# Three gate groups traced among branch C's tiles instead of branch A's

## The chip, the cores and the metric

The kernel runs on one core of one Trainium2 chip. The metric is the device time of one execution in microseconds (us). Three timed runs of the kernel before gave 2320.02, 2320.87 and 2327.75 us; their median, 2320.87 us, is what the changed kernel is compared with. The profile comes from a further execution, which took 2326.91 us.

## What is computed

Two transformer-like layers run one after the other on a sequence of 1024 tokens with 1024 features. The change lies in the first, which has four branches. Each branch yields y of 256 columns, which is gated, multiplied by a projection and weighted by a sigmoid gate taken from the layer's input h:

```
y_a = nsa_attention(...)               # branch A (index 0): compressed, selected and window attention
y_b = banded_attention(..., sink)      # branch B (index 1)
y_c = stick_breaking_attention(...)    # branch C (index 2): sigmoids and a cumulative product over the keys
y_d = retention(...)                   # branch D (index 3)
for i, (y, z) in enumerate(branches):
    yi = y * silu(z)
    term = sigmoid(h @ w_merge[i]) * (yi @ w_br[i])
    merged = term if merged is None else merged + term
x = x + gate * (merged @ w_out)
```

The selection in branch A picks 16 of 16 blocks at this length, so that its selected attention is causal attention over all keys. The second layer (a convolution, an attention, a pooling, an MLP) is not touched.

## The kernel before, in words

All large products are made three times over, with the operands split in a high and a low part (lines 229 to 231: high by high, high by low, low by high), each matmul 128 by 128 on 512 columns. Attention works in tiles of 128 queries. A branch treats its four heads as two pairs, and for each pair goes over eight tiles of queries, tile i seeing i+1 blocks of 128 keys. Tile (1, 5) below is pair 1, i = 5.

Branch A's tile (`tile_of` in `branch_a`) makes scores on TensorE (PE; L804, L806; for the compressed keys L1041, L1042), adds a bias and takes the maximum on VectorE (DVE; L845), exponentials on ScalarE (ACT; L857), the reciprocal and the normalisation on DVE (L865, L150), transposes on PE (L276), copies the transposed probabilities out as high part on ACT (L147) and low part on DVE (L157, tile PT), multiplies them with the values on PE (L823) and sums the result on DVE (L833, L834; `join`). It does so for the selected and for the window attention. Branch C's tile makes two sigmoids on ACT (L1108, L1109), masks on GpSimd (POOL; L1111), a scan on DVE (L1113), a product on DVE or POOL (L1115), and then the same transposes, copies and products.

Between the tiles stands work that does not depend on them: fillers. `attend` asks a table after each tile which to trace: `m` is one group of a merge (`fill`), `g` one gate group (`pre`), `q` the query products of pair 1, `z` the gate of a finished pair.

```
            for i in range(NT):
                with stream(_T["ST1"], -1000000):
                    tile_of(p, i, ops[p])
                for c in works.get((p, i), ""):
                    todo[c]()
```

The tables are `FA`, `FB` and `FC` in `_T`, for the branches A, B and C, and `FD` for branch D. A gate group works out sigmoid(h @ w_merge) ahead for one branch and a quarter of the columns: two weight loads of 512 KB (SP's queue) and their split in high and low parts (ACT, DVE, POOL), four products of 24 matmuls each into a PSUM bank named mm, a tanh on ACT for each, and a store of 256 KB to DRAM, which the merge loads later. The groups are taken in a fixed order from `pre_todo`: the four of branch A's gate, then branch C's. There are two mm banks; gate groups, merges and projections share them.

A scheduler places the instructions of each engine in one fixed order when the program is built. Tiles stand in a stream of higher priority, so that a filler goes where the tiles leave an engine free by the scheduler's own reckoning. The order of the branches is D, A, C, B. A merge is queued when its branch is done: that of A gives the fillers `m` of branch C. Where a gate has been worked out ahead, the merge makes only the product with w_br (6 matmuls in place of 24 more).

Of the kernel before, what the change touches and what calls it, by code (L numbers as in the profile page):

```python
# [17 lines left out]
P = 128  # L18
# [6 lines left out]
SLOPES = [2.0 ** -2, 2.0 ** -4, 2.0 ** -6, 2.0 ** -8]  # L25
QS = 0.125

_T = dict(STA='s', XN1=0, PWT=1, PO='0x1', PO2={}, PS=2, PSX=0, PSE='a', PB=99, PEA=(0, 1, 4), WB=8, XL=3, CLO='v', STE=None, STW=None, ST1='b', ST2='b', PLP='pvv', WLO2='v', QXP=1, LW='vp', LEAD=10, FD={0: 'g', 1: 'b', 6: 'g'}, FW=(0, 2), AG=0, PREO=(0, 2, 1), PMB=0, PWB=1, PM=3, SG=2, FA={(0, 2): 'g', (0, 3): 'mmm', (0, 7): 'qm', (1, 0): 'gg', (1, 6): 'gz'}, FB={(0, 3): 'm', (0, 7): 'qm', (1, 3): 'm', (1, 5): 'z', (1, 7): 'm'}, FC={(0, 3): 'mm', (0, 7): 'q', (1, 3): 'zm', (1, 6): 'm'}, NORM='v', NORM2='v', CS=4, CSB=8, MM=2, SB=2, TB=3, OB=1, WHI='aaav', WLO='pv', PTH='a', NW=9, NBLK=31, PTB=2, XN=1, AS=(2, 4, 6, 7), CPP=2, CALT=1, WORK='s0 A A A A A A A A p s1 q t c B c B c B c B c 0a 1a P w 5 4 6 7 g 2 3a e u c B e c B c e B c c e B 1b 0b 3b', KS=(2, 0, 3, 1))


_C1 = [("trel", 1024), ("wrel", 640), ("crel", 256), ("brel", 128), ("brel2", 128), ("dm", 512), ("xi", 256), ("zeta", 256)]
# [2081 lines left out]
```

## Time and profile before

| | us |
|---|---|
| median of three timed runs | 2320.87 |
| the profiled execution | 2326.91 |
| its span, first to last instruction | 2325.2 |
| PE busy in the span | 2239.4 |
| DVE busy in the span | 1517.2 |
| ACT busy, POOL busy | 966.2, 474.8 |

The span is what lies between the first and the last instruction that the profile records. A PE shown as busy is not at its peak: the next matmul starts before the one in front has ended. So what counts is the distance between starts, and an engine's idle time with what ended it. Branch A's tiles stand at about 279 to 640 us, branch C's at about 640 to 840 us, and branch B's follow.

### The profile page before, as it was taken

The page shows a single profiled execution, that of the slowest core. Times are in us where ns is not written, and L with a number is a line of the kernel's source. Part 1 is how long each engine was busy: PE and PEld are TensorE (multiplying, and loading weights), DVE is VectorE, ACT ScalarE, POOL GpSimd, SP SyncE. Part 2 cuts the span into 40 slices and gives each one's busy share as a digit, 9 for nine tenths or more (in the row PEclk, how much of TensorE's full clock was granted, in tenths as well). Part 3 has the DMA queues.
Part 4 walks back from the last instruction along what each step waited for, and adds up shares of the span by engine and source line. Part 5 has one row for each costly group of instructions (what it writes and reads, how often), then busy time and mean ns, then how long its engine had stood idle before and what let it go on. Part 6 is the DMA issues. An engine that isn't in the chain of part 4 may idle for free.

```text
span 2325.2 us, 30286 instructions
## 1 busy us (share of the span) xinstructions
PE 2239.4 (96%) x11004; PEld 1860.3 (80%) x11004; DVE 1517.2 (65%) x2955; ACT 966.2 (42%) x1941; POOL 474.8 (20%) x404
## 2 busy tenths in 40 slices
PE   8999999999989999999998999899999999999998
PEld 6788888888877778877887787677788888888877
DVE  7634466665677965623579876866576678578684
ACT  6211344444455544422322344634545454344452
POOL 4222100010155622112330000012034340000021
PEclk8999999999999999999999999999999999999999
DMA  9421221121132333224221211156565687525313
GB/s 319 165 90 61 63 69 50 46 89 62 32 109 84 116 119 106 73 82 145 103 71 28 82 50 37 37 172 212 159 192 180 203 324 248 176 90 163 109 55 118
DMA packets 202783, 272.72 MB, mean 117 GB/s; under 512 B 17086, under 2 KB 126214, under 8 KB 202634
## 3 DMA queue, kind: packets, MB, share of 16 engines
q1 hardware_dynamic: 194240, 257.95, 34.3%
q10 hardware_dynamic: 8394, 12.84, 1.8%
q8 instruction: 87, 1.43, 0.3%
q14 instruction: 62, 0.51, 0.1%
HBM read 199.43 MB, written 71.32 MB: 116 GB/s over the span
## 4 chain that ended last, share of the span: by engine, by line
PE 82%; DVE 9%; DMA 3%; ACT 2%; POOL 2%; issue 2%; SPq 0%; POOLq 0%; DVEq 0%; ACTq 0%
PE mm L229 15%; PE mm L230 15%; PE mm L231 15%; PE t L276 4%; PE o L823 3%; DVE blk L1342 2%; PE s L1682 2%; PE s L1684 2%; PE s L1683 2%; PE t L2028 1%; PE t L2029 1%; PE t L2027 1%; PE mm L2028 1%; PE t L1682 1%; PE mm L2029 1%
## 5 line engine op out<-in xcount | busy, mean ns | idle before, releaser
L229 PE MATMUL mm<-blk,wh 128*128 128x512 f32 x1264 | 506.2, 401 | 20.8 <-DVE tz L1157 6.2
L230 PE MATMUL mm<-blk,wh 128*128 128x512 f32 x1264 | 500.6, 396 | 0.0
L231 PE MATMUL mm<-blk,wl 128*128 128x512 f32 x1264 | 499.1, 395 | 0.3 <-DVE wl L157 0.3
L229 PEld LDWEIGHTS mm<-blk,wh 128*128 128x128 f32 x1264 | 238.7, 189 | 74.3 <-DVE tz L1157 9.2
L231 PEld LDWEIGHTS mm<-blk,wl 128*128 128x128 f32 x1264 | 238.7, 189 | 50.4 <-DVE wl L157 0.8
L230 PEld LDWEIGHTS mm<-blk,wh 128*128 128x128 f32 x1264 | 239.0, 189 | 45.9
L229 PE MATMUL mm<-wh,blk 128*128 128x512 f32 (+3 forms) x544 | 199.2, 368 | 4.3 <-DVE blk L149 1.9
L155 POOL TENSOR_TENSOR wl<-wr,wh 128x1024 fp32r<-128x1024 f32 (+1 forms) x43 | 104.5, 2431 | 465.0 <-ACT wh L147 265.4
L231 PE MATMUL mm<-wh,blk 128*128 128x512 f32 (+3 forms) x544 | 195.9, 361 | 0.3 <-DVE blk L157 0.3
L157 DVE SCALAR_TENSOR_TENSOR wh<-blk,wh 128x1024 fp32r<-128x1024 f32 x116 | 138.4, 1219 | 67.7 <-issue 59.9
L147 ACT ACTIVATE wh<-blk 128x1024 fp32r<-128x1024 f32 x116 | 117.1, 1053 | 156.1 <-PE s L2028 86.1
L230 PE MATMUL mm<-wl,blk 128*128 128x512 f32 (+3 forms) x480 | 172.2, 359 | 6.6 <-DVE wl L157 6.5
L147 ACT ACTIVATE blk<-mm 64x512 fp32r<-64x512 f32 (+3 forms) x138 | 77.8, 569 | 175.6 <-PE mm L231 112.9
L147 ACT ACTIVATE PT<-t 128x512 fp32r<-128x512 f32 (+3 forms) x224 | 96.1, 459 | 116.9 <-PE o L823 70.7
L147 ACT ACTIVATE wh<-wr 128x1024 fp32r<-128x1024 f32 (+2 forms) x95 | 97.8, 1032 | 104.4 <-DMA wr<-in_w_in_dram 25.1
L157 DVE SCALAR_TENSOR_TENSOR PT<-t,PT 128x512 fp32r<-128x512 f32 (+3 forms) x224 | 110.7, 513 | 38.9 <-ACT PT L147 38.2
L309 POOL TENSOR_TENSOR sm<-sm,mhalf 128x1 f32<-128x1 f32 x64 | 38.5, 604 | 444.0 <-DVE sm L308 425.3
L157 DVE SCALAR_TENSOR_TENSOR wl<-wr,wh 128x1024 fp32r<-128x1024 f32 (+2 forms) x76 | 96.8, 1273 | 41.1 <-ACT wh L147 18.1
L229 PEld LDWEIGHTS mm<-wh,blk 128*128 128x128 f32 x544 | 105.6, 194 | 20.7 <-DVE blk L149 2.1
L231 PEld LDWEIGHTS mm<-wh,blk 128*128 128x128 f32 x544 | 104.9, 193 | 16.2 <-DVE blk L157 1.0
L230 PEld LDWEIGHTS mm<-wl,blk 128*128 128x128 f32 x480 | 93.9, 196 | 20.4 <-DVE wl L157 8.3
L1158 POOL TENSOR_TENSOR acc<-tz,acc 128x512 f32<-128x512 f32 x48 | 67.8, 1416 | 157.7 <-DVE tz L1157 119.8
(364 smaller groups left out, 4847.5 us busy)
## 6 DMA issues: line engine op xcount, KB each, us to landing
acc<-acc SPq DMA_DIRECT2D x96, 256.0 KB, 2.6
wr<-in_w_merge_dram SPq DMA_DIRECT2D x32, 512.0 KB, 3.7
wu<-in_w_up_dram SPq DMA_DIRECT2D x32, 512.0 KB, 5.1
blk<-in_w_down_dram SPq DMA_DIRECT2D x32, 512.0 KB, 7.0
blk<-ss SPq DMA_DIRECT2D x32, 512.0 KB, 4.6
wr<-in_w_in_dram SPq DMA_DIRECT2D x27, 512.0 KB, 4.5
ss<-us SPq DMA_DIRECT2D x48, 256.0 KB, 2.3
blk<-sa SPq DMA_DIRECT2D x24, 512.0 KB, 4.4
```

The costliest lines, as they stand in the source:

```text
L147: return ac.activation(dst, src, AF.Copy, scale=1.0 if scale is None else scale)
L155: return po.tensor_tensor(lo, x, hi.bitcast(F32), op=ALU.subtract)
L157: return ve.scalar_tensor_tensor(out=lo, in0=x, scalar=scale, in1=hi.bitcast(F32), op0=ALU.mult, op1=ALU.subtract)
L229: pe.matmul(dst, sh, mh, start=(i == 0), stop=False)
L230: pe.matmul(dst, sh, ml, start=False, stop=False)
L231: last = pe.matmul(dst, sl, mh, start=False, stop=(i == n - 1))
L276: pe.transpose(dst, src, ident)
L823: behind_pe[0] = pe.matmul(dst, v(lo + c0 + j), PT[:, j].rearrange("p a q -> p (a q)"), start=start and c0 + j == 0, stop=stop and c0 + j ...
L1158: po.tensor_tensor(acc[:], t[:], acc[:], op=ALU.add)
L1342: ve.scalar_tensor_tensor(out=acc[:, c:c1], in0=u[:, c - l:c1 - l], scalar=w, in1=acc[:, c:c1], op0=ALU.mult, op1=ALU.add)
L1682: pe.matmul(dst, wh, xh, start=first and k == 0, stop=False, skip_group_check=True)
L1683: pe.matmul(dst, wh, xl, start=False, stop=False, skip_group_check=True)
```

## The change

Only the tables FA and FC are edited, within one long line.

```diff
...
-FA={(0, 2): 'g', (0, 3): 'mmm', (0, 7): 'qm', (1, 0): 'gg', (1, 6): 'gz'},
+FA={(0, 2): 'g', (0, 3): 'mmm', (0, 7): 'qm', (1, 6): 'z'},
...
-FC={(0, 3): 'mm', (0, 7): 'q', (1, 3): 'zm', (1, 6): 'm'},
+FC={(0, 1): 'g', (0, 3): 'mm', (0, 5): 'g', (0, 7): 'q', (1, 1): 'g', (1, 3): 'zm', (1, 6): 'm'},
...
```

The last group of branch A's gate and the first two of branch C's gate are traced after C's tiles (0, 1), (0, 5) and (1, 1) and no longer after A's tiles (1, 0) and (1, 6). Each still comes before the merge that uses it. The scheduler makes another order of it on all engines.

**On PE, in branch A's pair 1.** The rows begin with the product of tile (1, 4) with the compressed values (L1073) and belong to the tiles (1, 4) and (1, 5): s is a bank of scores, t one of transposes, o the tile's result, mm a bank of a filler. Before:

```order
L1073 MATMUL o_1037_5122<-cT_1042_5141,vc_2247 128x256
L823 MATMUL o_1037_5122<-PT_1064_5210,blk_437_2398 128x256 x4
L823 MATMUL o_1037_5122<-PT_1066_5219,blk_438_2399 128x256
L230 MATMUL mm_940_4757<-blk_166_817,wh_924_4662 128x512
L231 MATMUL mm_940_4757<-blk_165_816,wl_925_4663 128x512
L229 MATMUL mm_940_4757<-blk_165_816,wh_924_4662 128x512
L230 MATMUL mm_940_4757<-blk_166_817,wh_924_4662 128x512
L804 MATMUL s_1089_5312<-blk_422_2261,blk_842_4212 128x256
L806 MATMUL s_1089_5312<-blk_423_2262,blk_842_4212 128x256
L231 MATMUL mm_940_4757<-blk_165_816,wl_925_4663 128x512
L276 MATMUL t_1067_5223<-c2_63,blk_1054_5175 128x128 x4
L276 MATMUL t_1069_5235<-c2_63,blk_1054_5175 128x128
```

After the change, from the same instruction of the same tile on:

```order
L1073 MATMUL o_993_4866<-cT_998_4885,vc_2247 128x256
L823 MATMUL o_993_4866<-PT_1020_4954,blk_437_2398 128x256 x4
L823 MATMUL o_993_4866<-PT_1022_4963,blk_438_2399 128x256
L804 MATMUL s_1045_5056<-blk_422_2261,blk_842_4212 128x256
L806 MATMUL s_1045_5056<-blk_423_2262,blk_842_4212 128x256
L804 MATMUL s_1047_5061<-blk_422_2261,blk_843_4213 128x512
L806 MATMUL s_1047_5061<-blk_423_2262,blk_843_4213 128x512
L804 MATMUL s_1048_5065<-blk_422_2261,blk_843_4213 128x256
L806 MATMUL s_1048_5065<-blk_423_2262,blk_843_4213 128x256
L276 MATMUL t_1023_4967<-c2_63,blk_1010_4919 128x128 x4
L276 MATMUL t_1025_4979<-c2_63,blk_1010_4919 128x128
L276 MATMUL t_1027_4986<-c2_63,Pm_1003_4898 128x128 x4
```

Before, matmuls of a gate group (mm_940) stand between the parts of the tile. Now the tile's instructions follow each other, and so they do for 112 rows on from the instruction that makes the last scores of tile (1, 4): no matmul into an mm bank stands there.

**On DVE, near the end of branch A.** L157 on 64 rows and with mm as a source empties a bank of branch C's query products; PT, cT, Pm and o are of A's tiles. Before:

```order
L626 SCALAR_TENSOR_TENSOR tz_1248_6056<-tz_1248_6056,mm_1247_6031 128x512
L157 SCALAR_TENSOR_TENSOR PT_1162_5601<-t_1161_5596,PT_1162_5601 128x4x128
L157 SCALAR_TENSOR_TENSOR PT_1164_5610<-t_1163_5608,PT_1164_5610 128x128
L157 SCALAR_TENSOR_TENSOR cT_1202_5837<-t_1201_5835,cT_1202_5837 128x128
L157 SCALAR_TENSOR_TENSOR blk_1255_6076<-mm_1261_6084,blk_1255_6076 64x512
L157 SCALAR_TENSOR_TENSOR blk_1256_6077<-mm_1261_6084,blk_1256_6077 64x512
L833 TENSOR_REDUCE blk_868_4432<-o_1123_5450 64x128
L157 SCALAR_TENSOR_TENSOR PT_1224_5906<-t_1223_5901,PT_1224_5906 128x4x128
L833 TENSOR_REDUCE blk_868_4432<-o_1123_5450 64x128
L157 SCALAR_TENSOR_TENSOR PT_1226_5918<-t_1225_5913,PT_1226_5918 128x4x128
L834 TENSOR_TENSOR blk_868_4432<-blk_868_4432,ju_1165_5614 128x128
L157 SCALAR_TENSOR_TENSOR blk_1259_6080<-mm_1262_6113,blk_1257_6078 64x512
```

After the change:

```order
L157 SCALAR_TENSOR_TENSOR blk_1178_5615<-blk_868_4432,blk_1177_5614 128x512
L157 SCALAR_TENSOR_TENSOR PT_1110_5304<-t_1109_5299,PT_1110_5304 128x4x128
L157 SCALAR_TENSOR_TENSOR PT_1112_5313<-t_1111_5311,PT_1112_5313 128x128
L865 RECIPROCAL sm_1156_5511<-sm_1155_5508 128x2
L157 SCALAR_TENSOR_TENSOR blk_1189_5692<-mm_1195_5700,blk_1189_5692 64x512
L867 TENSOR_TENSOR sm_1156_5511<-sm_1156_5511,agate_778 128x2
L150 TENSOR_SCALAR blk_1148_5487<-blk_1148_5487,sm_1156_5511 128x640
L150 TENSOR_SCALAR blk_1151_5496<-blk_1151_5496,sm_1156_5511 128x640
L157 SCALAR_TENSOR_TENSOR blk_1190_5693<-mm_1195_5700,blk_1190_5693 64x512
L157 SCALAR_TENSOR_TENSOR blk_1193_5696<-mm_1196_5729,blk_1191_5694 64x512
L157 SCALAR_TENSOR_TENSOR PT_1114_5323<-t_1113_5318,PT_1114_5323 128x4x128
L157 SCALAR_TENSOR_TENSOR PT_1116_5334<-t_1115_5330,PT_1116_5334 128x3x128
```

In both, C's first query products wait in the mm banks until DVE has normalised the last tile of A. On PE these products now stand beside tile (1, 4), and the next filler is 116 rows behind the second of them; before, they stood behind tile (1, 7)'s scores.

**On PE, in branch C's pair 1.** s and t are tile work, o is a tile's result. Before:

```order
L276 MATMUL t_1469_7322<-c2_63,Pm_1467_7310 128x128 x2
L823 MATMUL o_1448_7242<-PT_1453_7258,cst_1265_6204 128x256
L823 MATMUL o_1448_7242<-PT_1458_7277,cst_1265_6204 128x256
L804 MATMUL s_1487_7392<-blk_1439_7115,blk_1437_7113 128x512
L806 MATMUL s_1487_7392<-blk_1441_7117,blk_1437_7113 128x512
L276 MATMUL t_1476_7350<-c2_63,Pm_1474_7338 128x128 x3
L229 MATMUL mm_1513_7540<-blk_1191_5754,wh_1506_7518 128x512
L230 MATMUL mm_1513_7540<-blk_1192_5755,wh_1506_7518 128x512
L231 MATMUL mm_1513_7540<-blk_1191_5754,wl_1507_7519 128x512
L229 MATMUL mm_1513_7540<-blk_1243_5998,wh_1506_7518 128x512
L230 MATMUL mm_1513_7540<-blk_1244_5999,wh_1506_7518 128x512
L231 MATMUL mm_1513_7540<-blk_1243_5998,wl_1507_7519 128x512
```

After the change:

```order
L804 MATMUL s_1487_7392<-blk_1417_6987,blk_1415_6985 128x512
L806 MATMUL s_1487_7392<-blk_1419_6989,blk_1415_6985 128x512
L231 MATMUL mm_1460_7249<-blk_142_663,wl_1455_7217 128x512
L229 MATMUL mm_1460_7249<-blk_142_663,wh_1454_7216 128x512
L823 MATMUL o_1438_7159<-PT_1443_7176,cst_1199_5820 128x256 x2
L230 MATMUL mm_1460_7249<-blk_143_664,wh_1454_7216 128x512
L276 MATMUL t_1476_7350<-c2_63,Pm_1474_7338 128x128 x3
L231 MATMUL mm_1460_7249<-blk_142_663,wl_1455_7217 128x512
L229 MATMUL mm_1464_7278<-blk_165_816,wh_1452_7212 128x512
L230 MATMUL mm_1464_7278<-blk_166_817,wh_1452_7212 128x512
L804 MATMUL s_1492_7417<-blk_1418_6988,blk_1416_6986 128x512
L823 MATMUL o_1438_7159<-PT_1448_7197,cst_1199_5820 128x256 x2
```

Beside the scores of the same tiles stood a merge's short products (mm_1513, 6 matmuls); now a gate group stands there (mm_1460 and mm_1464 are two of its four products of 24 matmuls), and the merge comes later.

## Rows read from the trace of the kernel before

**Rows 1.** The page: busy time by engine; the chain that ended last.

```profile
PE 2239.4 (96%) x11004; PEld 1860.3 (80%) x11004; DVE 1517.2 (65%) x2955; ACT 966.2 (42%) x1941; POOL 474.8 (20%) x404
PE 82%; DVE 9%; DMA 3%; ACT 2%; POOL 2%; issue 2%; SPq 0%; POOLq 0%; DVEq 0%; ACTq 0%
```

**Rows 2.** Windows: from:to, length, busy PE, PEld, DVE, ACT, POOL; clock, DMA.

```profile
534.00:557.00 23.00, 23.00 (x123) 19.67 (x123) 12.51 (x47) 9.67 (x25) 2.46 (x1) 1.00 0.27 81
557.00:585.00 28.00, 28.00 (x153) 24.02 (x151) 15.49 (x47) 10.93 (x24) 2.41 (x1) 1.00 0.21 66
585.00:640.00 55.00, 55.00 (x302) 47.33 (x301) 34.42 (x86) 27.58 (x60) 10.81 (x12) 1.00 0.09 26
640.00:695.00 55.00, 48.01 (x336) 43.62 (x335) 41.65 (x64) 28.24 (x69) 30.01 (x36) 0.98 0.36 110
695.00:745.00 50.00, 48.57 (x254) 41.04 (x253) 35.05 (x50) 27.68 (x61) 22.11 (x26) 0.98 0.24 79
745.00:815.00 70.00, 62.39 (x315) 51.03 (x314) 62.52 (x77) 38.90 (x85) 48.82 (x41) 0.95 0.36 113
815.00:850.00 35.00, 33.78 (x165) 27.56 (x164) 21.51 (x46) 15.44 (x34) 6.29 (x4) 1.00 0.29 93
```

**Rows 3.** Waits of PE at 640 to 835 us: us in total, times, longest.

```profile
PE o L823 <- DVE PT L157: 3.4, 2, 2.1
PE t L276 <- DVE Pm L1115: 2.7, 3, 1.7
PE mm L229 <- DVE tz L1157: 2.7, 3, 1.5
PE mm L229 <- DVE blk L157: 2.4, 2, 1.5
PE s L804 <- ACT blk L147: 1.4, 1, 1.4
```

**Rows 4.** Timeline of PE at 542 to 546 us: start, length, instruction, count.

```profile
542.10 0.39 PE L230 MATMUL mm<-blk,wh 128*128 128x512 f32 x1
542.33 0.39 PE L231 MATMUL mm<-blk,wl 128*128 128x512 f32 x1
...
545.10 0.78 PE L823 MATMUL o<-PT,blk 128*128 128x256 f32 x5
...
545.94 0.60 PE L276 MATMUL t<-c,blk 128*128 128x128 f32 x4
```

**Rows 5.** DVE's groups by form, 534 to 640 us: busy, mean ns; idle before.

```profile
L157 DVE SCALAR_TENSOR_TENSOR PT<-t,PT 128x512 fp32r<-128x512 f32 x16 | 11.0, 688 | 5.7 <-ACT PT L147 5.7
L845 DVE CUSTOM_DVE_ANT_0 Pm<-s,cst 128x512 f32<-128x512 f32 x8 | 5.5, 685 | 0.7 <-PE s L806 0.7
...
L150 DVE TENSOR_SCALAR blk<-blk,sm 128x640 f32<-128x640 f32 x8 | 4.1, 549 | 0.1
...
L833 DVE TENSOR_REDUCE blk<-o 64x128 f32<-64x256 f32 x6 | 2.5, 416 | 4.7 <-ACT ju L147 4.6
L157 DVE SCALAR_TENSOR_TENSOR PT<-t,PT 128x128 fp32r<-128x128 f32 x8 | 2.2, 279 | 0.0
...
L845 DVE DVE_READ_ACCUMULATOR2_ANT mx<- 128x1 f32 x24 | 2.0, 82 | 0.0
...
L865 DVE RECIPROCAL sm<-sm 128x2 f32<-128x2 f32 x7 | 1.2, 165 | 9.1 <-ACT blk L857 4.6 <-ACT Pm L857 4.5
```

**Rows 6.** Windows of 5 us in branch C and in the second layer's attention.

```profile
755.00:760.00 5.00, 4.31 (x13) 2.90 (x12) 4.94 (x7) 1.50 (x4) 4.92 (x6) 0.50 0.45 152
1435.00:1440.00 5.00, 2.82 (x12) 1.94 (x13) 4.81 (x17) 2.57 (x9) 0.68 (x1) 0.74 0.36 105
1440.00:1445.00 5.00, 4.21 (x18) 3.66 (x17) 4.56 (x17) 1.99 (x6) 0.55 (x1) 0.50 0.00 0
1445.00:1450.00 5.00, 4.00 (x22) 3.37 (x21) 4.90 (x20) 2.69 (x9) 0.59 (x1) 0.74 0.00 2
```

**Rows 7.** DMA issues: count, KB each, us to landing.

```profile
wr<-in_w_merge_dram SPq DMA_DIRECT2D x32, 512.0 KB, 3.7
```

More of the change, by code (lines that the diff above doesn't have):

```diff
@@ L26 @@
 QS = 0.125
-_T = dict(STA='s', XN1=0, PWT=1, PO='0x1', PO2={}, PS=2, PSX=0, PSE='a', PB=99, PEA=(0, 1, 4), WB=8, XL=3, CLO='v', STE=None, STW=None, ST1='b', ST2='b', PLP='pvv', WLO2='v', QXP=1, LW='vp', LEAD=10, FD={0: 'g', 1: 'b', 6: 'g'}, FW=(0, 2), AG=0, PREO=(0, 2, 1), PMB=0, PWB=1, PM=3, SG=2, FA={(0, 2): 'g', (0, 3): 'mmm', (0, 7): 'qm', (1, 0): 'gg', (1, 6): 'gz'}, FB={(0, 3): 'm', (0, 7): 'qm', (1, 3): 'm', (1, 5): 'z', (1, 7): 'm'}, FC={(0, 3): 'mm', (0, 7): 'q', (1, 3): 'zm', (1, 6): 'm'}, NORM='v', NORM2='v', CS=4, CSB=8, MM=2, SB=2, TB=3, OB=1, WHI='aaav', WLO='pv', PTH='a', NW=9, NBLK=31, PTB=2, XN=1, AS=(2, 4, 6, 7), CPP=2, CALT=1, WORK='s0 A A A A A A A A p s1 q t c B c B c B c B c 0a 1a P w 5 4 6 7 g 2 3a e u c B e c B c e B c c e B 1b 0b 3b', KS=(2, 0, 3, 1))
+_T = dict(STA='s', XN1=0, PWT=1, PO='0x1', PO2={}, PS=2, PSX=0, PSE='a', PB=99, PEA=(0, 1, 4), WB=8, XL=3, CLO='v', STE=None, STW=None, ST1='b', ST2='b', PLP='pvv', WLO2='v', QXP=1, LW='vp', LEAD=10, FD={0: 'g', 1: 'b', 6: 'g'}, FW=(0, 2), AG=0, PREO=(0, 2, 1), PMB=0, PWB=1, PM=3, SG=2, FA={(0, 2): 'g', (0, 3): 'mmm', (0, 7): 'qm', (1, 6): 'z'}, FB={(0, 3): 'm', (0, 7): 'qm', (1, 3): 'm', (1, 5): 'z', (1, 7): 'm'}, FC={(0, 1): 'g', (0, 3): 'mm', (0, 5): 'g', (0, 7): 'q', (1, 1): 'g', (1, 3): 'zm', (1, 6): 'm'}, NORM='v', NORM2='v', CS=4, CSB=8, MM=2, SB=2, TB=3, OB=1, WHI='aaav', WLO='pv', PTH='a', NW=9, NBLK=31, PTB=2, XN=1, AS=(2, 4, 6, 7), CPP=2, CALT=1, WORK='s0 A A A A A A A A p s1 q t c B c B c B c B c 0a 1a P w 5 4 6 7 g 2 3a e u c B e c B c e B c c e B 1b 0b 3b', KS=(2, 0, 3, 1))
 _C1 = [("trel", 1024), ("wrel", 640), ("crel", 256), ("brel", 128), ("brel2", 128), ("dm", 512), ("xi", 256), ("zeta", 256)]
```

## Prediction

> **What bounds the kernel now.** I read the page first, then windows cut at the branches, then what PE waits for, then DVE's work by form. The page shows PE busy for 2239.4 of 2325.2 us and carrying 82% of the chain that ended last, DVE 9% [rows 1]. So the time is PE's work plus its gaps, and since the change neither adds nor removes a matmul, it can act only through gaps and through the clock. The windows tell where the gaps are. In A's last tiles PE has none: it is busy for all 23, 28 and 55 us, at clock 1.00, while DVE is busy for 54%, 55% and 63% [rows 2]. In branch C PE is idle for 7.0 us at 640 to 695, 1.4 at 695 to 745 and 7.6 at 745 to 815, 16.0 us in all, and there DVE is busy for 76%, 70% and 89% [rows 2]. C's gaps end mostly on DVE's copies, scans' products and merges, a smaller part on the emptying of product banks [rows 3]. At first sight the change takes filler from where PE is full and gives it to where PE has gaps. What has to be asked is what A's tiles are without it.
>
> **What is moved.** A gate group is 4 products of 24 matmuls, 96 matmuls. Two of them start 0.23 us apart [rows 4], so a group is 22 us of PE and three are 66 us. With each go two weight loads (512 KB, 3.7 us to land, [rows 7]), two splits, four tanh on ACT and four stores. I cost all of these at nothing in branch A and at nothing in C: the loads are traced well ahead of their products and the DMA share of C's windows is 0.24 to 0.36 [rows 2], and ACT is busy for about half of C. The cover is thin for DVE alone: a split leaves it one or two instructions of a 1024-column tile, some 1.4 us each if twice the 512-column row [rows 5], so at most 3 groups by 2 by 1.4, 8 us, where DVE is idle for 36 us at 640 to 815 [rows 2].
>
> **What A loses.** In the new order PE has a run of 112 rows in tiles (1, 4) to (1, 7) without one filler. Its first 106 rows hold 55 transposes, 54 products with values, 12 short compressed scores and 24 pairs of scores over 9216 columns. By distances between starts, transposes cost (0.60-0.27)/3 = 0.11 us with 0.27 as the length of one alone, products (0.78-0.28)/4 = 0.125 us, a 512-column matmul 0.23 us [rows 4]; the 12 short ones I take as transposes. That is 6.1 + 6.8 + 1.3 + 8.2 = 22.3 us.
>
> In the same run DVE has to go through 147 instructions, from the maximum of the last scores of tile (1, 4) to the low part that PE's next row multiplies. By kind, with durations of [rows 5]:
> 27 of 512 columns (14 maxima, 10 low parts, 3 of finished halves) at 0.686 = 18.5;
> 15 of 128 columns at 0.28 = 4.2;
> 7 in between at about 0.48 = 3.4;
> 31 accumulator reads at 0.082 = 2.5;
> 12 normalisations of 640 columns or more at 0.549 or more = 6.6;
> 5 reductions at 0.416 = 2.1, and 3 additions, taken as 128 columns, 0.8;
> 35 on two columns at 0.165 = 5.8, 12 on 32 columns at no less = 2.0.
> The sum is 46 us. DVE takes them in this order, the first cannot start before PE has made its scores, and PE cannot go on without the last. So PE needs 46 us for 22.3 us of work: at least 24 us of new idle time, where now there is none. DVE will not be full either: where the second layer's attention runs with little filler, DVE is busy for 4.81, 4.56 and 4.90 of 5 us, 95% [rows 6]. 46/0.95 = 48, and the term is 26 us. Its bounds: 22 if a few short instructions are dearer in the rows than here, 34 if DVE also waits for ACT's exponentials, which end 9.1 us of DVE idle time before seven reciprocals now [rows 5], and nothing hides that without filler.
>
> Why there is no filler, while branch C's projections are still to do: C's first two query products now stand beside tile (1, 4), fill both mm banks and are emptied by DVE only after the last normalisation of tile (1, 7); the next product can't start earlier. That a bank, and not work, is missing makes it a hard stop.
>
> **What the clock adds.** Where PE had been idle for 44% of the time, at 1435 to 1440 us, the granted clock fell to 0.74 and then 0.50, which is the 1.2 GHz level, and was back after about 10 us; in C it stood at 0.50 at 755 to 760 [rows 6]. PE will be at 46% of its time in A's run. One such spell at half speed does 5 us less of PE work than at full, most of which hides behind DVE: I take 2 us, with bounds 0 and 22 (all of the run's 22.3 us at half speed, nothing hidden). The Trainium skill, "TensorE: Matmul & The Clock Gate", section "A second HAM failure mode: psum-queue depth-cycling", says that short idle spells between groups of matmuls can make the clock swing between half and full, and that throughput pays for it. Rows 6 agree, in C and in the second layer; by that page alone the run would sit at the low level again and again, which is the first rival.
>
> **What C gains.** PE's idle time there is 16.0 us [rows 2], so that is the upper bound; zero is the lower. I take 6. The waits for emptied banks, 2.4 and 1.4 [rows 3], stand at C's projections and at the start of pair 1, and there the new order has long stretches of filler ahead: 4 us go. The rest ends on DVE in tiles with a merge's short products between (3.4, 2.7 and 2.7), and these merges still stand beside C's late tiles, with DVE work as long as before: 2 of some 12 us go. Where the clock was at 0.95 and 0.98, 70 x 0.05 + 55 x 0.02 + 50 x 0.02 = 5.6 us of full clock are missing [rows 2]. The low spell at 755 to 760 stands at merges that stay, so I take 1.5 us as coming back (bounds 0 and 5.6). Stretches of C now hold filler alone; there PE is full and nothing is won or lost.
>
> **Sum.** 26 + 2 - 6 - 1.5 = 20.5 us. On the profiled execution, 2326.9 us, of which 2325.2 is the span and 1.7 lies around it, that gives 2347. The median is 6.0 us below that execution, so I predict 2320.87 + 20.5, about 2341 us, 0.9% slower.
>
> **Rivals.**
> First, PE at the 1.2 GHz level through A's run. For it: 44% of idle time was enough once [rows 6], and here it is half. Against: the clock came back in that attention although PE went on with gaps. The run's PE work would be 45 us beside DVE's 48, alternating rather than side by side; I put 15 us on top: 2356.
> Second, interleaving pays as the branch profile suggests: all 16 us of C's gaps and 3 us of its clock go, and A's run costs its lowest, 22 us or less because PE reaches it late and DVE early. That gives 2320.87 + 22 - 19 = 2324 or below, no change to be measured. For it: C's DVE is idle for 36 us. Against: two thirds of C's waits end on DVE's tile work, and this work stays.
> Third, it is faster: PE arrives at the run behind DVE by most of its length, so that the 46 us of DVE work started before PE needs it and costs at most 10 us, while C gains 19: 2312. It decides from a head start of DVE of 12 us. For it: DVE's share of 54% now [rows 2]. Against: the run's scores are made by PE inside the run, so DVE cannot have them earlier. The Trainium skill, "Perfetto Trace Analysis", section "Optimization Strategy", says that a kernel whose most contended engine changes between regimes may gain when the regimes are interleaved. That speaks for this outcome: A is PE's regime and C leans to DVE's. The windows agree on the regimes, yet what is moved leaves a DVE regime behind it.
> Fourth, C gets worse as well: the splits' DVE work (8 us) falls beside its late tiles where DVE is at 89%, and C gains nothing: 2320.87 + 28 + 4 = 2353.
>
> **Chances and range.** Forecast 0.66 (own range 2332 to 2352), clock 0.14, even 0.09, faster 0.04, C worse 0.07. A measurement of this kernel can tell about 0.3%, 7 us, from no change. Faster by more: 0.04, the third rival. Within: 0.08, nearly all of the second. Slower: 0.88. The range takes the unknown costs from the even case's edge, 2325, to the clock case, 2362.
>
> **What would show it.** Right: in A's pair 1 a stretch of about 50 us in which DVE is busy for over 90% and PE for about half, with PE's waits at transposes and value products on DVE's Pm, blk and PT, some 26 us in sum, and a granted clock below 1.00 in one or two windows; in C 10 us of PE idle time in place of 16; PE's count of matmuls unchanged. Wrong: PE full in A's last tiles, or its waits there ending on something other than DVE; C's idle time under 3 us, or above 16.

## The result

The changed kernel takes 2344.45 us (median of four runs, 2343.09 to 2344.91), against 2321.22 us for the kernel before in the same four rounds: 1.0093 of it, 95% interval 1.0074 to 1.0113. It is 23.2 us slower. The forecast was 20.5 us slower, 2341 us.

First the page of the changed kernel, which answers to [rows 1]: busy time by engine, then the chain that ended last.

```profile
PE 2246.5 (96%) x11004; PEld 1856.7 (79%) x11004; DVE 1506.3 (64%) x2955; ACT 966.8 (41%) x1941; POOL 468.0 (20%) x404
PE 82%; DVE 9%; DMA 4%; ACT 3%; issue 1%; POOL 1%; SPq 0%; DVEq 0%; POOLq 0%; ACTq 0%
```

The counts are the same and the shares nearly so: a page can't show where 20 us went. Next the windows of the changed kernel, with the columns of [rows 2], cut where its stages change: A's tiles with filler (461), the stretch without filler (527), A's end (567), branch C (602), C's first merges (650), a stretch between its pairs (696), pair 1 (736) and its merges (776).

```profile
461.00:527.00 66.00, 66.00 (x352) 56.13 (x350) 43.26 (x147) 28.40 (x80) 9.78 (x5) 1.00 0.20 61
527.00:567.00 40.00, 28.59 (x172) 21.68 (x170) 36.73 (x147) 25.64 (x69) 3.17 (x3) 0.99 0.00 1
567.00:602.00 35.00, 33.68 (x214) 30.46 (x215) 20.41 (x41) 19.11 (x43) 5.49 (x10) 0.91 0.10 31
602.00:650.00 48.00, 48.00 (x304) 43.03 (x303) 32.06 (x49) 25.73 (x60) 18.09 (x26) 1.00 0.11 39
650.00:696.00 46.00, 39.01 (x190) 31.03 (x189) 29.65 (x36) 17.72 (x37) 23.67 (x19) 0.93 0.57 183
696.00:736.00 40.00, 40.00 (x182) 32.98 (x181) 13.75 (x21) 14.85 (x29) 8.94 (x12) 1.00 0.19 59
736.00:776.00 40.00, 40.00 (x213) 34.00 (x212) 26.04 (x39) 22.73 (x54) 16.72 (x23) 1.00 0.23 74
776.00:817.00 41.00, 33.58 (x165) 26.86 (x163) 33.31 (x41) 17.63 (x36) 27.42 (x20) 0.92 0.50 154
```

In [rows 2] PE was busy for all of A's last tiles. Now there is a stretch of 40 us in which PE is busy for 28.59 and DVE for 36.73, 92%. In C, PE has 14.4 us of idle time, all of it in the two merge stretches (7.0 and 7.4), against 16.0 before; between them it is full. What PE waits for in A's tail of the changed kernel (527 to 602 us; us in total, times, longest) answers to no group, since PE did not wait there before:

```profile
PE o L823 <- DVE PT L157: 6.7, 5, 4.4
PE s L804 <- DVE mx L845: 3.3, 4, 2.2
PE s L804 <- ACT blk L147: 0.9, 1, 0.9
PE t L276 <- DVE PT L157: 0.6, 2, 0.4
```

All but 0.9 us of these waits end on DVE, as forecast. They make up 12.7 us of idle time by the windows, about half of the 26 us forecast, and the scores' wait for the maximum was not among the waits named. In C (602 to 817 us) three rows are on the same work as in [rows 3]; the two waits for copies out of product banks (DVE's blk, ACT's blk) are gone, and two others stand in their place:

```profile
PE o L823 <- DVE PT L157: 4.6, 3, 2.4
PE mm L229 <- DVE tz L1157: 2.5, 4, 0.9
PE t L276 <- DVE Pm L1115: 2.4, 4, 1.5
PE mm L229 <- DVE tz L626: 1.7, 1, 1.7
PE s L804 <- ACT Pm L1109: 1.7, 2, 1.1
```

**A measure that does not depend on modelled ends.** A busy PE may still wait, because the ends of matmuls are modelled. So I take from the timelines when PE starts the first matmul behind the last product with values (L823) of a pair of heads in a branch, and from the program's order which matmuls lie between two such starts. Their PE work is counted by distances between starts [rows 4]: 0.229 us for 512 columns, 0.108 for a transpose and for a score of 32 columns, 0.120 for a value product, others in proportion. Time less work is what PE lost. A's pair 1 in the changed kernel goes from 461.0 to 601.5 us, 140.6 us with 116.7 us of work: 23.9 lost. Before it went from 464.3 to 644.0, 179.8 with 177.5: 2.3 lost. The table holds these lost times in us for all kernels of this study (B is both of its pairs); the ratio is to the kernel before, from runs on the same chip (its median was 2323 to 2325 us in the later runs). The changed kernel's A was run three times over under different branches C and lost 23.9, 25.3 and 26.4, so a difference of 2 us in one profile says nothing.

| kernel | ratio, 95% interval | A pair 1 | C pair 0 | C pair 1 | B |
|---|---|---|---|---|---|
| before | 1 | 2.3 | 13.3 | 13.8 | 10.5 |
| changed | 1.0093, 1.0074 to 1.0113 | 23.9 | 13.4 | 13.3 | 11.0 |
| one group moved | 1.0069, 1.0048 to 1.0090 | 10.9 | 21.1 | 12.0 | 12.6 |
| two moved | 1.0097, 1.0080 to 1.0114 | 16.1 | 15.0 | 18.9 | 11.9 |
| A's half alone | 1.0020, 1.0008 to 1.0032 | 25.3 | 14.3 | 2.9 | 3.6 |
| C's half alone | 1.0187, 1.0168 to 1.0205 | 2.3 | 14.1 | 13.4 | 52.8 |
| one group, before C's merges | 1.0047, 1.0034 to 1.0061 | 11.6 | 10.0 | 16.9 | 10.5 |
| one more group between C's merges | 1.0097, 1.0082 to 1.0111 | 2.3 | 14.5 | 16.5 | 26.4 |
| one gate inside a merge of C | 1.0024, 1.0014 to 1.0035 | 10.8 | 12.4 | 2.9 | 12.0 |
| three gates inside merges of C | 1.0038, 1.0026 to 1.0050 | 26.4 | 5.6 | 2.1 | 11.9 |
| changed, normalisation on ACT | 1.0089, 1.0071 to 1.0107 | 25.3 | 10.0 | 13.4 | 11.5 |
| changed, no normalisation | 1.0065, 1.0051 to 1.0079 | 18.3 | 13.8 | 13.5 | 11.4 |
| last gate ahead, three groups | 1.0008, 0.9996 to 1.0019 | 2.2 | 14.2 | 2.8 | 2.8 |
| last gate ahead, four groups | 1.0066, 1.0050 to 1.0081 | 2.1 | 11.4 | 1.7 | 3.7 |

For the change: A +21.6, C -0.4, B +0.5, together 21.7 us. The two spans differ by only 17.2, because the profiled execution of before lost 3.3 us more ahead of A's pair 1, where both kernels do the same, and was itself 5.7 us above the median of its four runs.

### The profile page after: what moved, and what is told of

It is laid out like the page before. It is cut to its first block, busy times and chain, and to the rows that moved or that the text cites. A ratio compares the mean times of both kernels' runs of the same rounds, so it can differ in the third digit from the quotient of the medians.

```text
span 2342.4 us, 30284 instructions
## 1 busy us (share of the span) xinstructions
PE 2246.5 (96%) x11004; PEld 1856.7 (79%) x11004; DVE 1506.3 (64%) x2955; ACT 966.8 (41%) x1941; POOL 468.0 (20%) x404
## 4 chain that ended last, share of the span: by engine, by line
PE 82%; DVE 9%; DMA 4%; ACT 3%; issue 1%; POOL 1%; SPq 0%; DVEq 0%; POOLq 0%; ACTq 0%
PE mm L229 16%; PE mm L230 15%; PE mm L231 15%; PE t L276 3%; DVE blk L1342 3%; PE o L823 2%; PE s L1682 2%; PE s L1684 2%; PE s L1683 2%; PE t L2028 1%; PE t L2029 1%; PE t L2027 1%; PE mm L2028 1%; PE t L1682 1%; PE t L1684 1%
## 5 line engine op out<-in xcount | busy, mean ns | idle before, releaser
L157 DVE SCALAR_TENSOR_TENSOR wh<-blk,wh 128x1024 fp32r<-128x1024 f32 x116 | 138.7, 1222 | 67.0 <-issue 59.2
L157 DVE SCALAR_TENSOR_TENSOR PT<-t,PT 128x512 fp32r<-128x512 f32 (+3 forms) x224 | 110.8, 514 | 47.4 <-ACT PT L147 46.8
L157 DVE SCALAR_TENSOR_TENSOR wl<-wr,wh 128x1024 fp32r<-128x1024 f32 (+2 forms) x76 | 94.2, 1239 | 36.8 <-ACT wh L147 17.3
```

What stands on the lines that cost most here:

```text
L157: return ve.scalar_tensor_tensor(out=lo, in0=x, scalar=scale, in1=hi.bitcast(F32), op0=ALU.mult, op1=ALU.subtract)
```

## The experiments

Each diff shows only the tables that differ, `-` the changed kernel and `+` the experiment, unless it says otherwise.

**One group and two groups.**

```diff
-FA={(0, 2): 'g', (0, 3): 'mmm', (0, 7): 'qm', (1, 6): 'z'}
-FC={(0, 1): 'g', (0, 3): 'mm', (0, 5): 'g', (0, 7): 'q', (1, 1): 'g', (1, 3): 'zm', (1, 6): 'm'}
# one
+FA={(0, 2): 'g', (0, 3): 'mmm', (0, 7): 'qm', (1, 0): 'gg', (1, 6): 'z'}
+FC={(0, 3): 'mm', (0, 7): 'q', (1, 1): 'g', (1, 3): 'zm', (1, 6): 'm'}
# two
+FA={(0, 2): 'g', (0, 3): 'mmm', (0, 7): 'qm', (1, 0): 'g', (1, 6): 'z'}
+FC={(0, 3): 'mm', (0, 5): 'g', (0, 7): 'q', (1, 1): 'g', (1, 3): 'zm', (1, 6): 'm'}
```

> Only the last of the three groups (the one at A's tile (1, 6)) goes to branch C, the two at (1, 0) stay. Theory 'starved tail': the time goes where PE has no filler beside A's last tiles and DVE sets the pace. After the change that stretch lost 18 us for 24 us of PE work without a filler; here the longest stretch of that kind holds 10.7 us of PE work, so it should lose about 8 us: 2329 us. Rival 'branch C': the loss is made by what the groups displace in C, so it goes by what C receives at its tile (1, 1), one group of three: 2321 + 23/3 = 2329 us, but with A's tail as full as before and the loss in C. The place of the lost time tells the two apart, not the total.

> Two groups go to branch C, one stays at A's tile (1, 0). Theory 'starved tail': the stretch without a filler holds 17.8 us of PE work (24.2 with three moved), so 18.3/24.2 x 17.8 = 13 us are lost there and a few beside it: 2334 to 2337 us. Rival 'clock': the loss comes with the fall of the granted clock once PE idles for long; then the second group costs little or nothing over the first, or the whole step of 23 us comes at once, 2344 us.

Measured 1.0069 and 1.0097, 16 and 22 us. A's part came as expected: 10.9 - 2.3 = 8.6 us and 13.8 us, against 21.6 with three groups, for 10.7, 17.8 and 24.2 us of PE work without a filler. So A's loss grows with the length of that stretch, with no step of a clock in it. The total does not: C lost 6 us more than before with one group and 6.8 with two, and 0.4 less with three. What a group does in C was clearly not understood.

**A's half alone.** The groups are taken out of A and put nowhere, so that later merges work out these gates themselves.

```diff
-FC={(0, 1): 'g', (0, 3): 'mm', (0, 5): 'g', (0, 7): 'q', (1, 1): 'g', (1, 3): 'zm', (1, 6): 'm'}
+FC={(0, 3): 'mm', (0, 7): 'q', (1, 3): 'zm', (1, 6): 'm'}
```

> The three groups are taken out of branch A and put nowhere: the merges that need these gates work them out themselves, one in branch C, two in branch B. Branch A is as in the changed kernel, branch C's tiles get their fillers as in the kernel before. Theory 'starved tail': 2341 to 2347 us, no better than the changed kernel, with some 23 us lost in A's last tiles. Rival 'branch C': C's new order is what costs; then this kernel is near 2321 to 2330 us.

Measured 1.0020, some 5 us, which is what the rival said, and yet A lost its 25.3 us. My theory was right on A and wrong on the total: C's pair 1 lost 2.9 us in place of 13.8 and B 3.6 in place of 10.5. That gave 18 us back, and no kernel that puts the groups among C's tiles had won any of it.

**C's half alone.** A as before, C as in the changed kernel; three further gates are worked out ahead, two of merges that run in B and one of the last merge, which had made them themselves.

```diff
# against the kernel before
-FC={(0, 3): 'mm', (0, 7): 'q', (1, 3): 'zm', (1, 6): 'm'}
+FC={(0, 1): 'g', (0, 3): 'mm', (0, 5): 'g', (0, 7): 'q', (1, 1): 'g', (1, 3): 'zm', (1, 6): 'm'}
```

> Branch A keeps its three groups as in the kernel before; branch C's tiles (0, 1), (0, 5) and (1, 1) get three further groups, which the later merges in branches C and B would otherwise work out themselves. With the kernel that did the other half (groups taken out of A, put nowhere: 1.002 of before) and the changed kernel (1.009) this makes a square of four. Theory 'no place beside a tile': A's tail is full, C loses 27 us as before and as after the change, since most of the added products stand where no tile is; 2321 to 2329 us. Rival 'sum of halves': the groups in C cost by themselves what the first half did not show, 2324 + 17 = 2341 us.

Measured 1.0187, 43 us, worse than either theory. C lost 27.5, as expected (14.1 and 13.4), and A 2.3. The loss is in B: 52.8 us. Here are the windows of B, first of the kernel before, then of this one with its largest waits of PE:

```profile
826.00:994.00 168.00, 160.29 (x788) 132.79 (x786) 100.31 (x291) 73.86 (x209) 39.57 (x27) 1.00 0.35 109
```

```profile
867.00:1033.00 166.00, 135.92 (x595) 106.45 (x594) 105.22 (x297) 69.78 (x202) 37.59 (x26) 0.88 0.36 112
```

```profile
PE t L276 <- DVE Pm L150: 12.2, 9, 2.2
PE mm L229 <- DVE tz L1157: 7.2, 6, 1.7
```

B's tiles do the same work in the same time, with 43 us less PE work in it (113.3 in place of 156.7 us, by distances between starts); that work was done in C instead, where it won nothing. PE is idle for 30 of the 166 us, and at a granted clock of 0.88 another 166 x 0.12 = 20 us of full clock are missing, an estimate. Two things meet here and are not told apart: the tiles have less filler, as in A's tail, with waits that end on their normalisation (L150), and all four merges in B are now short, two in the kernel before, with waits that end on the merge (L1157).

**The place in C.** One group traced in front of C's first merges (taken from A), and one between them (in addition, A untouched).

```diff
# in front, against the kernel with one group moved
-FC={(0, 3): 'mm', (0, 7): 'q', (1, 1): 'g', (1, 3): 'zm', (1, 6): 'm'}
+FC={(0, 3): 'gmm', (0, 7): 'q', (1, 3): 'zm', (1, 6): 'm'}
# between, against the kernel before
-FC={(0, 3): 'mm', (0, 7): 'q', (1, 3): 'zm', (1, 6): 'm'}
+FC={(0, 3): 'mgm', (0, 7): 'q', (1, 3): 'zm', (1, 6): 'm'}
```

> As the kernel with one group moved, but the group is traced in front of C's first two merges, at tile (0, 3), and not at (1, 1). On PE 11 us of long products without a tile between them disappear from the end of C. Theory 'place beside a tile': A's tail loses the same 9 us, C loses 24 to 28 us in place of 33: 2330 to 2336 us against 2342. Rival 'the group itself costs': what it adds in C (weights, splits, stores) does not hang on the place: 2342 us.

> The kernel before with one further gate group, traced between C's first two merges; A is untouched, a later merge finds its gate worked out. Theory 'place beside a tile': C's short merge products get 22 us of long products among them and C loses up to 8 us less; branch B loses these long products between its own merges and may give a part back: 2314 to 2324 us. Rival 'merges set by DVE': the time of C's merge stretches is DVE's and POOL's work, products between make no difference: 2322 to 2328 us.

The first: 1.0047, C 26.9 in place of 33.1, as expected. The place counts for 6 us in C; in the time it is 5 us, and the two intervals overlap. C still gains nothing on before. The second: 1.0097, 22 us slower, and C lost 31.0, more than before, though on PE the group does stand between the first four short products and the next four; B, with 16 us less PE work, lost 26.4. Both theories fell: long products traced between merges do not help. What is left of the kernel without the groups is that there a merge makes its own gate.

**Gates inside the merges.** The groups given up by A are in no table; the list of gates to work out ahead skips those of merges that run in C.

```diff
# one: FA of the kernel with one group moved, FC of before; three: FA of the changed kernel, FC of before
-    pre_d, pre_todo = {}, [(b, g) for b in _T["PREO"] for g in range(4)]
+    pre_d, pre_todo = {}, [(b, g) for b in _T["PREO"] for g in range(4) if (b, g) != (0, 3)]   # one
+    pre_d, pre_todo = {}, [(b, g) for b in _T["PREO"] for g in range(4) if b or not g]         # three
```

> Branch A gives up one gate group, as in the kernels with one group moved (at C's tile (1, 1): 1.007 of before; in front of C's first merges: 1.005). Here the group is not traced among C's tiles at all: the last merge in branch C works out that gate itself, so that each of its four short products of 6 matmuls follows one of 24. Branch B finds as much filler as before. Theory 'short merges': C's gaps come from merge products of 1.4 us that each need DVE and a bank, and only long products between them help, as in the kernel without the groups, where C lost 10 us less. A's tail loses 9 us, C loses 8 to 11 us less than 27: 2319 to 2328 us, no change. Rival 'one more group in C costs, wherever it stands': 2336 to 2342 us.

> Branch A gives up three gate groups as in the changed kernel, and C gets the same 66 us of products, but inside its merges: three of the four merges in branch C work out their gates themselves. Theory 'short merges': A's tail loses 22 to 24 us as in the changed kernel; of C's 27 us 10 to 20 go: 2325 to 2337 us. Rival 'C is limited by its tiles': C loses 27 us whatever is given to it, 2344 us.

Measured 1.0024 and 1.0038 against 1.0069 and 1.0093 of the kernels that give up as much in A. C lost 15.3 and 7.7 us in place of 27.1; with three, A still lost 26.4. That is the theory's side, inside its range with three and a microsecond above it with one: 12 and 19 us come back in C. The two merges of pair 1 show it best. In the kernel before both are short and stand in one window:

```profile
745.00:778.00 33.00, 28.12 (x140) 22.92 (x139) 30.70 (x45) 20.49 (x48) 28.32 (x27) 0.90 0.47 152
```

With one gate inside, the short one stands at 729 to 741 us and the one with its gate behind it:

```profile
729.00:741.40 12.40, 11.12 (x57) 8.49 (x55) 10.43 (x18) 8.60 (x18) 10.65 (x12) 1.00 0.44 127
745.00:778.00 33.00, 33.00 (x180) 28.17 (x179) 23.75 (x33) 17.19 (x43) 16.20 (x18) 1.00 0.32 104
```

From the first short product to the last these merges lost 9.7 us before and 2.8 with one gate inside, 2.4 of it in the merge that is still short. In the other PE is busy throughout and the clock is at 1.00: DVE's and POOL's steps per product, the two loads and the store now have 7 us of PE work beside them (24 + 6 matmuls) and not 1.4. One gate inside should have come out even (A +8.5, C -11.8, B +1.5); the time is some 6 us above before. Its profile shows 4 us more lost in the second layer than that of before, though the change does not touch it; that part varied by 6 us among the profiles, and why stays open.

**What holds the tail up.** The 16 normalisations of A's tiles (1, 4) to (1, 7) on ACT, and then left out.

```diff
             copy(Ps[hh][:, :n * P], Ps[hh][:, :n * P], pick("norm", norm or _T["NORM"]), rd[:, hh:hh + 1])
...
-                               nsl, hd, weight=gw(1))
+                               nsl, hd, weight=gw(1), norm='a' if p == 1 and i >= 4 else None)
...
```

> The changed kernel with the 16 normalisations of A's tiles (1, 4) to (1, 7) on ACT in place of DVE. Theory 'starved tail', DVE sets the pace: 12 of them fall in the stretch without filler, at 0.549 us or more each on DVE, 6.6 us or more; PE's lost time there falls by about as much: 2336 to 2339 us. Rival 'clock' or PE's own latency: DVE is only busy, not the limit; no change, 2344 us. Rival 'ACT': the exponentials and copies of the same tiles queue behind them and it gets no better or worse, 2344 to 2350 us.

> The changed kernel without the 16 normalisations of A's tiles (1, 4) to (1, 7); they are left out, so the attention of these tiles is not divided by its sums. With them on ACT, DVE was busy 28 of 40 us in A's tail and no time was won. Theory 'two queues': DVE with them and ACT with them is each the fuller engine; without them on either the tail loses 6 us or more less, 2335 to 2340 us. Rival 'chain': PE waits for the steps of one tile after another (scores, maximum, exponential, transposes, copies) and for the banks, not for a full engine; then at most the 2 us of the last link are won: 2342 to 2346 us.

The windows of the stretch, on ACT and then without:

```profile
527.00:567.00 40.00, 29.86 (x170) 22.56 (x171) 30.14 (x130) 32.23 (x78) 2.84 (x3) 0.96 0.00 1
```

```profile
527.00:567.00 40.00, 31.94 (x202) 25.91 (x202) 35.11 (x144) 28.77 (x77) 3.18 (x3) 0.95 0.00 1
```

On ACT: 1.0089, A lost 25.3. DVE fell from 36.73 to 30.14 us of 40 and ACT rose from 25.64 to 32.23, and no time was won; that DVE alone sets the pace is disproved. PE's longest waits there (527 to 602 us) still end on DVE's low parts, which come behind ACT's high parts:

```profile
PE o L823 <- DVE PT L157: 9.9, 8, 3.3
```

Left out: 1.0065, A lost 18.3, 5.6 to 8.1 us less than the three of the same order, the theory of two queues' side. With the steps on neither engine the stretch does get shorter, so they lie on the way from scores to values wherever they stand. Whether a fuller queue or the steps' own length counts, these runs don't tell apart.

**A version meant to beat both.** The six groups stay in D and A, but three (or four) are of the gate whose merge comes last, behind all tiles.

```diff
# against the kernel before
-    pre_d, pre_todo = {}, [(b, g) for b in _T["PREO"] for g in range(4)]
+    pre_d, pre_todo = {}, [(0, 0), (0, 1), (0, 2), (1, 0), (1, 1), (1, 2)]             # three
+    pre_d, pre_todo = {}, [(0, 0), (0, 1), (1, 0), (1, 1), (1, 2), (1, 3)]             # four
```

> The kernel before with its six gate groups in their places in D and A, but three of the six are now of branch B's gate, whose merge comes last, behind all tiles, in place of one of A's and two of C's. So A's tiles keep their filler, one merge in C and two in B work out their gates themselves, and the short products stand where no tile is. Theory 'short merges': A loses 2 us, C 10 us less than before, B 7 us less (as in the kernel without the three groups); the last merge has 12 short products, each with 1.4 us of DVE beside 1.4 us of PE, which may lose 0 to 10 us: 2305 to 2317 us against some 2323. Rival 'conserved': gaps only move, the last merge loses what C and B win, 2320 to 2328 us.

> As the other kernel, with four of the six groups of branch B's gate: two merges in C and two in B work out their gates, all of the last merge is short. Theory 'short merges': C loses 16 to 19 us less than before, B 7 less, the last merge with its 16 short products loses 0 to 14: 2298 to 2314 us. Rival 'conserved': 2320 to 2330 us.

Measured 1.0008, no change, which is the rival's side, and 1.0066, slower than the rival had it too. With three groups C and B came as expected (17.0 and 2.8: 18 us won), but up to the end of the last merge 15 us more were lost than before (18.8 against 3.4). With four it was 32 (40.1 against 8.0, counted 50 us of PE work further on): 22 in the merge and 10 at the start of the products behind it, whose weights were not ready. So short merge products cost as much where no tile stands beside them. Windows of the last merge of the kernel with four, two waits of PE and two of POOL (1030 to 1100 us), and some of its timeline (start, length, instruction, idle time before and what ended it):

```profile
1010.00:1040.00 30.00, 26.83 (x115) 20.62 (x113) 12.35 (x16) 8.90 (x13) 7.39 (x5) 0.99 0.46 148
1040.00:1070.00 30.00, 19.13 (x60) 13.20 (x60) 14.39 (x19) 6.90 (x11) 12.72 (x10) 0.83 0.57 172
```

```profile
PE mm L229 <- DVE tz L1157: 15.4, 8, 4.5
PE mm L229 <- ACT wh L147: 5.3, 1, 5.3
POOL acc L1158 <- DMA acc<-acc: 24.7, 9, 7.6
POOL acc L1158 <- DVE tz L1157: 6.9, 2, 3.5
```

```profile
1049.97 2.30 SPq L1142 DMA_DIRECT2D acc<-acc  x2
...
1053.11 1.30 POOL L1158 TENSOR_TENSOR acc<-tz,acc 128x512 f32<-128x512 f32 x1 [3.72 <-DMA acc<-acc]
...
1055.78 1.26 POOL L1158 TENSOR_TENSOR acc<-tz,acc 128x512 f32<-128x512 f32 x1 [1.37 <-DMA acc<-acc]
...
1057.47 1.29 SPq L1142 DMA_DIRECT2D acc<-acc  x2
1058.34 0.68 DVE L1157 SCALAR_TENSOR_TENSOR tz<-tz,mm 128x512 f32<-128x512 f32 x1
1059.77 0.69 DVE L1157 SCALAR_TENSOR_TENSOR tz<-tz,mm 128x512 f32<-128x512 f32 x1 [0.76 <-DMA tz<-pre]
...
1063.69 2.46 SPq L1142 DMA_DIRECT2D acc<-acc  x2
```

DVE is busy for 14.39 of 30 us and POOL for 12.72, so neither is full. The sums' loads go out in pairs, 7.5 and 6.2 us apart, one pair when the pair before has been added, and for each pair PE has 2.8 us of work at full clock; the clock granted in this window was 0.83. `acc` and `tz` have two buffers each. That the two buffers set this pace is read from the rows and was not tried with a third. In C's merge stretches DVE is busy for 93% (30.70 of 33 us above), and whether DVE or the buffers count there stays open.

## Why the prediction was right, and where it was not

**A's tail: right in place and kind, the size too high.** Forecast were 26 us and 2 for the clock, bounds 22 and 34; 21.6 came, just under the bounds. The stretch without filler, DVE above 90% and PE's waits on DVE's PT and the like are there, in the windows and waits above. The term that was mis-sized is DVE's 46 us, a sum of durations [rows 5], raised to 48 for a share of 95%. Instructions of DVE overlap in the records, as these of the changed kernel show:

```profile
553.76 0.16 DVE L865 RECIPROCAL sm<-sm 128x2 f32<-128x2 f32 x1
553.84 0.17 DVE L1046 CUSTOM_DVE_ANT_0 cs<-s,cst 128x32 f32<-128x32 f32 x1
553.93 0.08 DVE L1046 DVE_READ_ACCUMULATOR2_ANT sm<- 128x1 f32 x1
553.93 0.19 DVE L1046 CUSTOM_DVE_ANT_0 cs<-s,cst 128x32 f32<-128x32 f32 x1
554.04 0.08 DVE L1046 DVE_READ_ACCUMULATOR2_ANT sm<- 128x1 f32 x1
554.04 0.69 DVE L845 CUSTOM_DVE_ANT_0 Pm<-s,cst 128x512 f32<-128x512 f32 x1
554.65 0.08 DVE L845 DVE_READ_ACCUMULATOR2_ANT mx<- 128x1 f32 x1
```

The first six have 1.37 us of durations in 0.89 us. The 147 instructions of DVE that start at 527 to 567 us, as many as the forecast counted, have durations of 46.9 us in sum, and DVE is busy for 36.73 us there. I had counted PE by distances between starts and DVE by durations. And the cause was told too simply: DVE was nearly full, but not the limit by itself, as the run with the normalisation on ACT showed. That a bank, and not work, was missing for the next filler agrees with the trace. The last matmul of C's first two query products starts at 526.1 us; the last copy out of the first one's bank is the first of the two instructions at 569.74, and the next query product starts behind it:

```profile
567.78 0.68 DVE L157 SCALAR_TENSOR_TENSOR blk<-mm,blk 64x512 fp32r<-64x512 f32 x1
569.74 1.41 DVE L157 SCALAR_TENSOR_TENSOR blk<-mm,blk 64x512 fp32r<-64x512 f32 x2
570.49 0.79 PE L229 MATMUL mm<-blk,wh 128*128 128x512 f32 x1
```

PE's order is fixed, too, and no kernel with a third bank was run, so this is agreement and not a test.

**The clock.** It was 0.99 and 0.91 in the two windows of A's tail, so the first rival, the whole stretch at the low level, did not come. By the windows, 40 x 0.01 + 35 x 0.09 = 3.6 us of full clock are missing there, an estimate near the 2 us forecast; what it cost within the 21.6 us was not separated.

**C's gain: wrong.** Forecast were 6 us of gaps and 1.5 of clock, and 0.4 came. The waits for emptied banks, 2.4 and 1.4 us [rows 3], did go. The step that failed is to count them, and 2 us of tile waits, as won, with no others in their place: the waits on DVE's PT grew from 3.4 to 4.6 us, waits of 1.7 us each on tz (L626) and on ACT's Pm came up, and idle time fell only from 16.0 to 14.4 us. Nor did the clock come back: 46 x 0.07 + 41 x 0.08 = 6.5 us of full clock are missing in the windows, 5.6 before. In the new order 28.4 us of filler stand on PE between the last value product of C's pair 0 and the first work of a tile in pair 1, and another 27.5 us behind the last one; the longest such run before was 7.9 us. PE's value products alone in three windows show it (length, PE, PEld, clock, DMA):

```profile
650.00:696.00 46.00, 7.67 (x47) 6.58 (x47) 0.93 0.57 183
696.00:736.00 40.00, 0.00 (x0) 0.00 (x0) 1.00 0.19 59
736.00:776.00 40.00, 4.70 (x30) 4.53 (x30) 1.00 0.23 74
```

The prediction did say that such a stretch is full and wins nothing, and did not ask how much of the 66 us it would take. Nor did it ask what the merges cost. C's gaps are mostly theirs: in the kernel before, some 11 of PE's 16 us of idle time in C lie between the first and the last short product of a pair. All four merges of C still find their gates worked out, and only a gate inside a merge took gaps away.

**The sum.** A came out 6.4 us under the forecast (with the clock), C 7.1 over, B 0.5 over: the errors cancelled, and that the total came within 3 us of the forecast is luck. The rival by which C gets worse as well had its price in the kernels with one and two groups, 6 us, though not in the change itself. Interleaving, the second and third rivals, could win in C only what stands inside the merges.

## What to carry to other kernels

Work that is moved as filler has two accounts, and the branch that it leaves must be asked first: tiles whose steps alternate between engines lose as soon as PE has nothing else, here 0.8 to 0.9 us for each us of PE work in the stretch without filler. Look in the new order for how much of the filler stands beside a tile at all, and ask what the gaps at its new place are made of: products worked out ahead leave short products behind, and here most of the gaps stood among those. When one engine is counted by distances between starts, count the others so too.

## What was not expected of the hardware

In A's tail DVE at 92% was not the limit by itself: with 6.6 us of its work moved to ACT, DVE stood at 75% and ACT at 81%, and the time stayed. And products of 6 matmuls, 1.4 us each, whose results are joined with two tiles that come by DMA into two buffers each, followed each other every 3.1 to 3.8 us, with DVE and POOL each under half busy and the granted clock at 0.83.
